# A two-layer hybrid decoder trunk: the instruction order comes from the framework's finer model, and layer 0's output projection multiplies three of its four chunk groups in three passes

## The chip, the cores and the metric

The kernel runs on one core of one Trainium2 chip. The metric is the device time of one execution in microseconds (us). The kernel before takes 2581.92 us, the median of three runs (2581.72 to 2582.03).

## What is computed

One sequence of 256 tokens, width 2048, goes through two layers. All arrays are float32. Each layer has a token mixer and a feed-forward part (FFN), both normalised and then shifted, scaled and gated by six vectors that a conditioning vector `c` gives. The mixer projects to 4888 columns, runs three mixers on their shares of the columns, and projects the joined results back.

```python
def reference(x, c, positions, w_mod, b_mod, ...):
    c_act = jax.nn.silu(c)
    for l in range(DEPTH):                                  # 2 layers
        mod = c_act @ w_mod[l] + b_mod[l]                   # 2048 x 12288 per layer
        shift1, scale1, gate1, shift2, scale2, gate2 = jnp.split(mod[:, None, :], 6, axis=-1)
        h = rms_norm(x, norm1_gain[l]) * (1.0 + scale1) + shift1
        x = x + gate1 * hybrid_token_mixer(h, ...)
        h = rms_norm(x, norm2_gain[l]) * (1.0 + scale2) + shift2
        x = x + gate2 * swiglu_ffn(h, ffn_w_gate[l], ffn_w_up[l], ffn_w_down[l])
    return rms_norm(x, final_norm_gain)

def hybrid_token_mixer(h, ..., w_in, ..., w_out):
    (aq, ak, av, ag, alr, bq, bk, bv, cq, ck, cv, cz, cb, ca) = _split_columns(h @ w_in, IN_SIZES)
    o_a = ...   # gated linear attention, 4 heads
    o_b = ...   # sliding-window softmax attention, 16 heads
    o_c = ...   # gated DeltaNet, 4 heads: short convolution, then a triangular solve per chunk
    return jnp.concatenate([o_a, o_b, o_c], axis=-1) @ w_out

def swiglu_ffn(h, w_gate, w_up, w_down):                    # 2048 -> 5632 -> 2048
    return (jax.nn.silu(h @ w_gate) * (h @ w_up)) @ w_down
```

## The kernel before

Everything is written once, unrolled, in one function `trunk`, about 18,400 instructions. The 256 tokens are two blocks (`blk`) of 128 rows. Each projection is a `stream` of jobs: a job is one row block `k` of 128 weight rows by up to 1024 columns. SyncE's queue (SP) loads it (`raw`, 512 KB, line 323); then there are two ways to multiply it.

- **Three passes.** ScalarE (ACT) copies `raw` to a rounded part `wh` (L330), VectorE (DVE) subtracts to get the remainder `wl` (L331), and TensorE (PE) multiplies the activations' parts `xh` and `xl` with them: three matmuls for each block and 512 columns (L358).
- **Whole.** The unsplit float32 row block is multiplied by unsplit float32 activations: one matmul in the program for each block and 512 columns, which the trace records as two. Nothing is split on ACT or DVE, and `raw` rotates through the nine buffers `raw`, `wh`, `wl` and not three.

`stream` chooses by the set `whole`:

```python
            if k in whole:
                terms = ((lhs(k, blk, True), 0),)
            else:
                xh, xl = lhs(k, blk, False)
                terms = ((xh, 0), (xh, 1), (xl, 0))
```

Layer 0's input projection is whole in all but 13 jobs of the columns from 0 and the 16 of the columns from 1024; layer 1 has nothing whole. The output projection has four groups of four row blocks: group 0 holds the gated linear attention (GLA), 1 and 2 the softmax attention, 3 DeltaNet. It first runs the row blocks 4 to 15 (groups 1 to 3), which do not need GLA, with GLA's own steps among them, and then the blocks 0 to 3. `to_mix` and `split_mix` keep a group's activations whole, or split them (ACT copy, DVE subtraction on L393), by `WHOLE_OUT[l]`.

**The modulation.** `mod = c_act @ w_mod` has one row, so it is not a matmul: SP loads 512 KB pieces (`mraw`, two buffers, L220) and DVE multiplies and adds each piece into `acc` (L223, 128x1024). The first pieces of layer 0, which the first normalisation needs, are 256 KB and go through the buffers `g`. A finished sum is turned by PE (L248) and DVE (L250 to L256) into columns, or by L238 into a gate's row. In the code, `tick` writes these pieces between the jobs, at rates set by constants, so the 448 pieces (320 of 512 KB, 128 of 256 KB) are spread over both layers.

**The DeltaNet recurrence.** For each of six sizes and two blocks there is a chain: PE L678, DVE L680, PE L685, DVE L686, PE L403 (transpose), ACT L687, and behind it further steps to L735. The softmax attention is L895, L898 to L906, L911, L916, L920 for each set of heads.

**What sets the order.** The code's order gives priorities only. The framework (`TileContext`) walks a model of the core and puts on each engine the ready instruction of highest priority, then writes the waits. Each engine, and SP's queue, has its own list in that order.

Of the kernel before, what the change touches and what calls it, by code (L numbers as in the profile page):

```python
# [42 lines left out]
WHOLE_IN = (True, False)  # L43
WHOLE_A = (3, 0)
RATE_LAST = 1.6
WHOLE_OUT = ((0, 1, 2, 3), ())
XN_ACT = ((False, False), (False, False))

FIN_LAG = 4
# [54 lines left out]
def trunk(ctx: ExitStack, tc, x, cT, pos, small, consts, b_mod, w_mod, w_in, w_gk, w_out,  # L104
# [272 lines left out]
    def ahead(wsp_n, hm_n):  # L377
        return (None,) * wsp_n + (at_hm,) * hm_n
# [7 lines left out]
    def split(src, scale=None):  # L386

        h = tl(hmp, [P, 4, P], "hm", F32R)
        lo = tl(hmp, [P, 4, P], "hm", F32R)
        h2, lo2 = (t.rearrange("p a b -> p (a b)") for t in (h, lo))  # L390
        if scale is None:
            A.activation(h2, src, AF.Copy)
            V.tensor_tensor(lo2, src, h2.bitcast(F32), ALU.subtract)  # L393
        else:
            A.activation(h2, src, AF.Copy, scale=scale)
            V.scalar_tensor_tensor(lo2, src, scale, h2.bitcast(F32), ALU.mult, ALU.subtract)
        return h, lo
# [91 lines left out]
    def to_mix(l, key, ps, gain=None):  # L489
        if key[1] == 0 and 0 not in WHOLE_OUT[l]:  # L490
            mix[key] = split(ps, gain)
            return
        t = mix[key] if key in mix else tl(hmp, [P, 4, P], "hm")
        A.activation(t.rearrange("p a b -> p (a b)"), ps, AF.Copy,
                     scale=1.0 if gain is None else gain)
        mix[key] = t
# [23 lines left out]
    def split_mix(l, group):  # L520
        if group not in WHOLE_OUT[l]:
            for blk in range(NB):
                mix[blk, group] = split(mix[blk, group].rearrange("p a b -> p (a b)"))
# [425 lines left out]
    def layer(l):  # L949
# [158 lines left out]
        for ks in (range(4, 16), range(0, 4)):  # L1108
            final = ks[0] == 0
            if final:  # L1110
# [3 lines left out]
                           blk, j, ps, half, final)) for half in range(2)]  # L1114
            stream(groups, ks, lhs_mix, whole=[k for k in ks if k // 4 in WHOLE_OUT[l]],
                   tail=() if not final else TAIL_WHOLE if 0 in WHOLE_OUT[l] else
                   ahead(*TAIL_OUT))
# [100 lines left out]
```

## Time and profile before

| | |
|---|---|
| median of three runs | 2581.92 us |
| the profiled execution | 2585.34 us, of which 2583.5 us are the span of instructions |
| PE busy | 2432.7 us (94%), 11,164 records |
| DVE busy | 1714.4 us (66%) |
| ACT busy | 1053.5 us (41%) |
| moved by DMA | 600.79 MB, 233 GB/s over the span |

The stages stand in the trace, by the first matmul of each, at: 40.8 us layer 0's input projection (the normalisation uses its first modulation before that); 238 us the columns that run beside DeltaNet's and the softmax attention's steps; 408 us layer 0's output projection with GLA; 566 us layer 0's FFN; 1372 us layer 1's mixer; 1816 us layer 1's FFN; the last matmul ends near 2566 us. The program has 10,120 matmuls and transposes on PE.

In the rows that follow, a busy share counts an engine's instructions; PEclk is the granted TensorE clock as a share of full speed, and the DMA share is the mean busy share of the core's 16 DMA engines.

### The profile page before, as it was taken

What the parts mean: (1) busy time and instruction counts of PE and PEld (TensorE: products, weight loads), DVE (VectorE), ACT (ScalarE), POOL (GpSimd) and SP (SyncE); (2) the same over time, 40 slices, a digit from 0 to 9 for tenths busy, and PEclk for the clock granted to TensorE, in tenths of its full rate; (3) what the DMA queues carried; (4) which work ended last, traced back from release to release, by engine and by line L of the source; (5) the groups of instructions that cost most, each with busy time, mean ns of one, the idle gap of its engine ahead of it and who ended that gap; (6) DMA issues with size and microseconds to landing.
All of it is one profiled execution on the core that took longest, in us unless ns stands there. A gap on an engine that the chain in (4) does not pass through costs nothing.

```text
span 2583.5 us, 30803 instructions
## 1 busy us (share of the span) xinstructions
PE 2432.7 (94%) x11164; PEld 1884.1 (73%) x11164; DVE 1714.4 (66%) x2171; ACT 1053.5 (41%) x1548; POOL 58.2 (2%) x117
## 2 busy tenths in 40 slices
PE   4999998889999988999999999999999999999998
PEld 2555785447878767788877878877778878888876
DVE  6767867576675777657578785888664575544555
ACT  2203443124444333344335454564644434344443
POOL 1000000000000000000000000000000000000000
PEclk9999999989999999999999999999999999999999
DMA  9996538777778888868687861675676686666654
GB/s 341 368 322 204 180 114 282 258 231 268 261 259 260 283 268 274 292 193 286 223 277 261 281 192 50 214 232 192 212 256 193 200 286 195 188 191 188 189 184 155
DMA packets 190033, 600.79 MB, mean 233 GB/s; under 512 B 21628, under 2 KB 26268, under 8 KB 189496
## 3 DMA queue, kind: packets, MB, share of 16 engines
q1 hardware_dynamic: 189880, 598.81, 70.7%
q8 instruction: 88, 1.44, 0.2%
q14 instruction: 65, 0.53, 0.1%
HBM read 596.63 MB, written 2.10 MB: 232 GB/s over the span
## 4 chain that ended last, share of the span: by engine, by line
PE 57%; DMA 20%; DVE 10%; issue 8%; ACT 4%; POOL 1%; SPq 1%; DVEq 0%; ACTq 0%; POOLq 0%
PE acc L358 48%; DMA mraw<-in_w_mod 13%; DVE wl L331 4%; DMA raw<-in_w_down 3%; DMA raw<-in_w_in 2%; DVE acc L223 2%; ACT wh L330 1%; PE mm L403 1%; PE ga L895 1%; DMA raw<-in_w_up 1%; PE mm L678 1%; PE mm L685 1%; PE ga L916 1%; DMA raw<-in_w_gate 1%; PE fin L248 1%
## 5 line engine op out<-in xcount | busy, mean ns | idle before, releaser
L358 PE MATMUL acc<-wh,hm 128*128 128x512 f32 (+3 forms) x4872 | 1339.2, 389 | 20.9 <-DVE xs L931 4.7
L330 ACT ACTIVATE wh<-raw 128x1024 fp32r<-128x1024 f32 (+3 forms) x669 | 684.7, 1025 | 985.8 <-PE acc L358 548.9
L331 DVE TENSOR_TENSOR wl<-raw,wh 128x1024 fp32r<-128x1024 f32 (+3 forms) x669 | 785.2, 1179 | 446.6 <-ACT wh L330 444.5
L358 PEld LDWEIGHTS acc<-wh,hm 128*128 128x128 f32 x4872 | 892.0, 189 | 215.8 <-issue 25.5
L358 PE MATMUL acc<-wl,hm 128*128 128x512 f32 (+3 forms) x2484 | 792.3, 394 | 12.2 <-DVE wl L331 9.7
L223 DVE SCALAR_TENSOR_TENSOR acc<-mraw,c_act,acc 128x1024 f32<-128x1024 f32 x320 | 410.3, 1282 | 225.2 <-DMA mraw<-in_w_mod 222.9
L358 PEld LDWEIGHTS acc<-wl,hm 128*128 128x128 f32 x2484 | 458.4, 190 | 124.1 <-DVE wl L331 22.3
L358 PE MATMUL acc<-wh,ahl 128*128 128x512 f32 x560 | 158.4, 397 | 0.0
L358 PEld LDWEIGHTS acc<-wh,ahl 128*128 128x128 f32 x560 | 105.8, 189 | 24.5
L358 PE MATMUL acc<-wl,ahl 128*128 128x512 f32 x280 | 90.8, 398 | 7.2 <-DVE wl L331 7.2
L223 DVE SCALAR_TENSOR_TENSOR g<-g,c_act,g 128x512 f32<-128x512 f32 x128 | 88.7, 747 | 12.6 <-DMA g<-in_w_mod 12.4
L358 PE MATMUL acc<-wh,b 128*128 128x512 f32 (+2 forms) x184 | 74.7, 545 | 2.2 <-ACT b L447 2.1
L358 PE MATMUL acc<-wl,b 128*128 128x512 f32 (+2 forms) x176 | 67.1, 518 | 2.6 <-DVE g L969 2.6
L358 PEld LDWEIGHTS acc<-wl,ahl 128*128 128x128 f32 x280 | 52.2, 189 | 23.1 <-DVE wl L331 11.3
L358 PE MATMUL acc<-raw,b 128*128 128x512 f32 (+2 forms) x176 | 67.6, 524 | 0.0
L358 PEld LDWEIGHTS acc<-wh,b 128*128 128x128 f32 x184 | 35.2, 197 | 30.8 <-issue 23.1
L358 PEld LDWEIGHTS acc<-wl,b 128*128 128x128 f32 x176 | 32.8, 192 | 29.2 <-issue 20.3
L416 ACT ACTIVATE acc<-xs 128x512 f32<-128x512 f32 x32 | 19.0, 595 | 85.7 <-DVE xs L931 85.7
L447 ACT ACTIVATE b<-mm,mod,mod 128x128 f32<-128x128 f32 x24 | 9.2, 461 | 109.7 <-DVE mod L256 92.1
L358 PEld LDWEIGHTS acc<-raw,b 128*128 128x128 f32 x176 | 33.5, 195 | 26.7 <-issue 21.7
L929 DVE TENSOR_TENSOR acc<-acc,gate 128x512 f32<-128x512 f32 x64 | 43.0, 695 | 10.3 <-PE acc L358 10.2
L358 PE MATMUL acc<-raw,hm 128*128 128x512 f32 x88 | 41.7, 598 | 1.4 <-ACT acc L416 1.4
(314 smaller groups left out, 1645.8 us busy)
## 6 DMA issues: line engine op xcount, KB each, us to landing
mraw<-in_w_mod SPq DMA_DIRECT2D x320, 512.0 KB
raw<-in_w_down SPq DMA_DIRECT2D x176, 512.0 KB
raw<-in_w_gate SPq DMA_DIRECT2D x160, 512.0 KB
raw<-in_w_up SPq DMA_DIRECT2D x160, 512.0 KB
raw<-in_w_in SPq DMA_DIRECT2D x72, 512.0 KB
g<-in_w_mod SPq DMA_DIRECT2D x128, 256.0 KB
raw<-in_w_out SPq DMA_DIRECT2D x43, 512.0 KB
raw<-in_w_in SPq DMA_DIRECT2D x32, 264.0 KB
```

Of the source, the lines that this page charges most:

```text
L223: V.scalar_tensor_tensor(acc, raw[:, a], c_act[:, i + a:i + a + 1], acc, ALU.mult, ALU.add)
L248: TE.transpose(ps[:, i * P:(i + 1) * P], acc[:, (j + i) * P:(j + i + 1) * P], ident)
L330: A.activation(wh[:, :width], raw[:, :width], AF.Copy)
L331: V.tensor_tensor(wl[:, :width], raw[:, :width], wh[:, :width].bitcast(F32), ALU.subtract)
L358: TE.matmul(ps[blk, j][:, :segs[j][2]], xa, parts[j][part], start=i == 0 and n == 0, stop=last and n == len(terms) - 1)
L403: TE.transpose(ps[:, j * P:(j + 1) * P], src[:, j * P:(j + 1) * P], ident)
L416: A.activation(scr[0]() if junk is None else junk, xs[:, blk, j * 512:(j + 1) * 512], AF.Square, accum_out=ssq[blk][:, j:j + 1])
L678: TE.matmul(ps[:, s], LT[blk][:, s], Tm[blk][:, s], start=True, stop=True)
L685: TE.matmul(ps[:, s], U[blk][:, s], m1[:, s], start=True, stop=True)
L895: TE.matmul(ps[:, j * nk:(j + 1) * nk], qT[rows, i + j], kT[rows, g, :nk], start=True, stop=True)
L916: TE.matmul(ps[:, j * 64:(j + 1) * 64], pT[:, j * nk + kb * P:j * nk + (kb + 1) * P], kv[kb][:, P + g * 64:P + (g + 1) * 64], start=kb == ...
L929: V.tensor_tensor(ps, ps, need(gate_row, (l, part, j)), ALU.mult)
```

## The change

Two edits. The order of all instructions now comes from the framework's other, finer model of the core. And in layer 0's output projection only group 0 (GLA) stays whole; the groups 1 to 3 take three passes, so 96 whole matmuls become 288, 24 jobs get a `wh` and a `wl`, and six activation tiles get a split.

```diff
--- before.py
+++ after.py
@@ -43,7 +43,7 @@
 WHOLE_IN = (True, False)
 WHOLE_A = (3, 0)
 RATE_LAST = 1.6
-WHOLE_OUT = ((0, 1, 2, 3), ())
+WHOLE_OUT = ((0,), ())
 XN_ACT = ((False, False), (False, False))
 
 FIN_LAG = 4
@@ -1211,7 +1211,7 @@
         args.append(nc.dram_tensor(f"in_{n}", a.shape, mybir.dt.from_np(a.dtype),
                                    kind="ExternalInput").ap())
     args.append(nc.dram_tensor("out_0", (T, D), F32, kind="ExternalOutput").ap())
-    with tile.TileContext(nc) as tc:
+    with tile.TileContext(nc, schedule_with_timeline_sim=True) as tc:
         trunk(tc, *args)
     r = run_bass_kernel_spmd(nc, [named], core_ids=[0])
     return r.results[0]["out_0"].reshape(1, T, D)
```

The edits' reach is seen in the order. On SP at the start of the program, before (`g` in L220: first modulation pieces, 256 KB; `wh_347`, `wl_372`: buffers that hold whole row blocks of the input projection, L323):

```order
L220 DMA g_295<-in_w_mod 128x512
L220 DMA g_298<-in_w_mod 128x512
L220 DMA g_301<-in_w_mod 128x512
L220 DMA g_313<-in_w_mod 128x512
L323 DMA wh_347<-in_w_in 128x1024
L213 DMA g_357<-in_b_mod 1x512
L220 DMA g_360<-in_w_mod 128x512
L213 DMA g_363<-in_b_mod 1x512
L220 DMA g_366<-in_w_mod 128x512
```

and now:

```order
L220 DMA g_232<-in_w_mod 128x512
L323 DMA wh_347<-in_w_in 128x1024
L323 DMA wl_372<-in_w_in 128x1024
L323 DMA raw_387<-in_w_in 128x1024
L323 DMA wh_402<-in_w_in 128x1024
L323 DMA wl_424<-in_w_in 128x520
L220 DMA g_235<-in_w_mod 128x512
L323 DMA raw_437<-in_w_in 128x520
L220 DMA g_238<-in_w_mod 128x512
L220 DMA g_241<-in_w_mod 128x512
L323 DMA wh_449<-in_w_in 128x520
L220 DMA g_244<-in_w_mod 128x512
```

Before, the first weight block followed the last of the 32 pieces that the first normalisation needs. Now ten weight loads, and a little later four 512 KB pieces of the first gate's modulation, are queued ahead of the last of them: 16.6 MB stand in the list up to that piece, 10.9 MB before.

On PE in layer 0's DeltaNet recurrence (L678, L685, L403), before (`acc` from `wh`, `wl`: the input projection's columns from 0; `ga` from `consts`: the softmax attention's transposes):

```order
L678 MATMUL mm_1719<-g_1693,g_1681 128x128 x4
L358 MATMUL acc_2497<-wh_2608,hm_993 128x512
L358 MATMUL acc_2498<-wh_2608,hm_993 128x512
L358 MATMUL acc_2493<-wh_2629,hm_657 128x512
L358 MATMUL acc_2494<-wh_2629,hm_657 128x512
L358 MATMUL acc_2493<-wl_2630,hm_657 128x512
L685 MATMUL mm_1726<-g_1724,g_1690 128x128 x4
L358 MATMUL acc_2494<-wl_2630,hm_657 128x512
L911 MATMUL ga_2191<-consts_88,b_2178 128x128 x2
L358 MATMUL acc_2493<-wh_2629,hm_658 128x512
L911 MATMUL ga_2191<-consts_88,b_2178 128x128 x2
L358 MATMUL acc_2494<-wh_2629,hm_658 128x512
```

and now:

```order
L678 MATMUL mm_1719<-g_1693,g_1681 128x128 x4
L895 MATMUL ga_2255<-kT_1425,b_2170 128x256 x2
L248 MATMUL fin_3783<-consts_88,acc_3481 128x128 x4
L685 MATMUL mm_1726<-g_1724,g_1690 128x128 x4
L248 MATMUL fin_3789<-consts_88,acc_3481 128x128 x4
L403 MATMUL mm_1732<-consts_88,g_1693 128x128 x4
L678 MATMUL mm_1738<-g_1650,g_1638 128x128 x4
L911 MATMUL ga_2266<-consts_88,b_2253 128x128 x4
L916 MATMUL ga_2272<-kv_533,b_2265 128x64
L916 MATMUL ga_2272<-kv_538,b_2265 128x64
L916 MATMUL ga_2272<-kv_533,b_2265 128x64
L916 MATMUL ga_2272<-kv_538,b_2265 128x64
```

The projection's matmuls have gone: they now stand ahead of the recurrence. Between the last matmul of the input projection and the first of the output projection there were 7 instructions on PE, and now there are 326; in layer 1, 6 and now 192.

On DVE at the same place, before:

```order
L680 TENSOR_TENSOR g_1724<-mm_1719,masks_90 128x512
L901 TENSOR_REDUCE low_590_2184<-b_2178 128x2
L223 SCALAR_TENSOR_TENSOR acc_2032<-mraw_2666,c_act_102,acc_2032 128x1024
L686 TENSOR_TENSOR g_1693<-g_1693,mm_1726 128x512
L906 RECIPROCAL tot_591_2186<-tot_591_2186 128x2
L331 TENSOR_TENSOR wl_2672<-raw_2669,wh_2671 128x1024
L223 SCALAR_TENSOR_TENSOR acc_2032<-mraw_2687,c_act_102,acc_2032 128x1024
L680 TENSOR_TENSOR g_1743<-mm_1738,masks_90 128x512
L920 TENSOR_TENSOR b_2177<-ga_2197,tot_591_2186 128x2x64
L223 SCALAR_TENSOR_TENSOR acc_2032<-mraw_2708,c_act_102,acc_2032 128x1024
```

and now:

```order
L680 TENSOR_TENSOR g_1724<-mm_1719,masks_90 128x512
L223 SCALAR_TENSOR_TENSOR acc_3691<-mraw_3694,c_act_102,acc_3691 128x1024
L898 TENSOR_TENSOR b_2253<-ga_2255,masks_90 128x2x256
L250 TENSOR_REDUCE sums_960_3782<-fin_3783 128x4
L686 TENSOR_TENSOR g_1693<-g_1693,mm_1726 128x512
L223 SCALAR_TENSOR_TENSOR acc_3691<-mraw_3715,c_act_102,acc_3691 128x1024
L901 TENSOR_REDUCE low_611_2259<-b_2253 128x2
L250 TENSOR_REDUCE sums_960_3782<-fin_3789 128x4
L223 SCALAR_TENSOR_TENSOR acc_3691<-mraw_3718,c_act_102,acc_3691 128x1024
L680 TENSOR_TENSOR g_1743<-mm_1738,masks_90 128x512
```

Modulation pieces (L223) now stand between almost all steps of the recurrence, 41 of them beside those 326 PE instructions; before, the steps shared DVE with fewer pieces and with the projection's splits (L331).

On SP in layer 0's FFN, at the loads of `w_down`, before:

```order
L220 DMA mraw_6710<-in_w_mod 128x1024
L323 DMA raw_6317<-in_w_down 128x1024
L220 DMA mraw_6767<-in_w_mod 128x1024
L323 DMA raw_6335<-in_w_down 128x1024
L220 DMA mraw_6806<-in_w_mod 128x1024
L323 DMA raw_6356<-in_w_down 128x1024
L323 DMA raw_6374<-in_w_down 128x1024
L220 DMA mraw_6863<-in_w_mod 128x1024
L323 DMA raw_6395<-in_w_down 128x1024
L220 DMA mraw_6902<-in_w_mod 128x1024
```

and now:

```order
L220 DMA mraw_8539<-in_w_mod 128x1024
L323 DMA raw_6590<-in_w_down 128x1024
L220 DMA mraw_8578<-in_w_mod 128x1024
L323 DMA raw_6611<-in_w_down 128x1024
L220 DMA mraw_8635<-in_w_mod 128x1024
L323 DMA raw_6629<-in_w_down 128x1024
L220 DMA mraw_8674<-in_w_mod 128x1024
L323 DMA raw_6647<-in_w_down 128x1024
L213 DMA acc_10057<-in_b_mod 1x1024
L323 DMA raw_6668<-in_w_down 128x1024
```

Pieces and weights now alternate one to one. Counted over SP's whole list, the 512 KB pieces stand as follows; the bytes in all are the same.

| stage (SP's list, from its first weight load) | before | now |
|---|---|---|
| layer 0 up to its output projection | 47 | 56 |
| layer 0's output projection | 42 | 40 |
| layer 0's FFN | 135 | 192 |
| layer 1's mixer | 64 | 0 |
| layer 1's FFN | 32 | 32 |

## The prediction

> **What bounds the kernel now.** I read the page's busy times, the windows by stage, the chain of waits, and the timeline at the places that the order moves. The page, and the chain's shares by engine:
>
> ```profile
> span 2583.5 us, 30803 instructions
> PE 2432.7 (94%) x11164; PEld 1884.1 (73%) x11164; DVE 1714.4 (66%) x2171; ACT 1053.5 (41%) x1548; POOL 58.2 (2%) x117
> PE 57%; DMA 20%; DVE 10%; issue 8%; ACT 4%; POOL 1%; SPq 1%; DVEq 0%; ACTq 0%; POOLq 0%
> by line: PE acc L358 48.4%; DMA mraw<-in_w_mod 12.7%; issue 7.9%; DVE wl L331 4.0%; DMA raw<-in_w_down 2.8%; DMA raw<-in_w_in 2.3%; DVE acc L223 2.1%; ACT wh L330 1.2%; PE mm L403 1.1%; PE ga L895 0.9%; DMA raw<-in_w_up 0.9%; PE mm L678 0.8
> ```
>
> PE is the bound where it is dense; where it waits, it mostly waits for modulation pieces (`mraw`), which no matmul reads but which stand in DVE's list and SP's list ahead of what one does read. The windows show which stage has room (columns: PE, PEld, DVE, ACT and POOL busy, granted clock, DMA share, GB/s):
>
> ```profile
> 36.00:165.00 129.00, 125.34 (x388) 70.06 (x388) 92.15 (x155) 20.43 (x48) 2.73 (x16) 1.00 1.01 365
> 220.00:410.00 190.00, 181.28 (x1083) 143.56 (x1082) 141.60 (x276) 88.36 (x202) 11.72 (x17) 0.96 0.52 165
> 408.00:558.00 150.00, 136.23 (x463) 66.01 (x463) 103.42 (x137) 27.44 (x57) 5.89 (x5) 0.98 0.82 274
> 558.00:566.00 8.00, 2.23 (x8) 1.43 (x8) 7.93 (x13) 4.27 (x11) 0.55 (x1) 0.71 0.80 272
> 566.00:1372.00 806.00, 768.68 (x3354) 617.38 (x3355) 543.38 (x522) 330.74 (x383) 10.00 (x12) 0.98 0.78 258
> 861.00:1016.00 155.00, 140.57 (x604) 110.68 (x603) 108.68 (x102) 53.63 (x53) 1.90 (x2) 0.99 0.84 275
> 1200.00:1245.00 45.00, 45.00 (x206) 37.24 (x205) 32.09 (x31) 19.34 (x21) 0.00 (x0) 1.00 0.86 286
> 1372.00:1816.00 444.00, 422.22 (x2434) 348.85 (x2434) 344.51 (x547) 233.53 (x431) 18.41 (x35) 0.99 0.62 200
> 1816.00:2566.00 750.00, 738.34 (x3265) 603.35 (x3264) 415.63 (x399) 324.73 (x370) 1.28 (x2) 1.00 0.65 206
> ```
>
> The start (36 to 165) is full of transfers: share 1.01. The recurrences of layer 0 (220 to 410) leave the DMA half empty, yet keep PE at 95%. The same FFN takes 806 us in layer 0, with 135 pieces, and 750 us in layer 1, with 32.
>
> **The passes.** In the timeline and in a dense stretch of the chain:
>
> ```profile
> 47.33 3.60 PE L358 MATMUL acc<-wl,b 128*128 128x512 f32 x8
> 50.76 3.60 PE L358 MATMUL acc<-raw,b 128*128 128x512 f32 x8
> 1112.83 50.38 PE acc L358 x222
> ```
>
> Eight records, that is four whole matmuls, start 3.43 us after the four before: 0.858 us each. A pass takes 50.38/222 = 0.227 us, three 0.681. So 96 x (0.858 - 0.681) = 17 us of PE go. The price is 24 more ACT copies and DVE subtractions of a row block and six of an activation tile:
>
> ```profile
> L330 ACT ACTIVATE wh<-raw 128x1024 fp32r<-128x1024 f32 x605 | 640.5, 1060 | 918.6 <-PE acc L358 526.0 <-DMA raw<-in_w_down 118.8 <-DMA raw<-in_w_up 104.6
> L331 DVE TENSOR_TENSOR wl<-raw,wh 128x1024 fp32r<-128x1024 f32 x605 | 736.7, 1223 | 435.6 <-ACT wh L330 434.3
> ```
>
> A job now holds PE for 12 x 0.227 = 2.7 us; 1.06 us of ACT and 1.22 us of DVE hide under that, and DVE gets rid of this stage's pieces. The tile splits fall among the last DeltaNet steps. GLA's end loses cover: its last normalisation now has eight whole matmuls beside it, where more stood before. These small losses and the pieces' absence I set against each other: -18 us for the stage, between -30 (its 14 us of idle PE go too) and 0 (GLA's chain becomes the bound).
>
> **The start.** DVE and SP there:
>
> ```profile
> 5.32 26.05 SPq L220 DMA_DIRECT2D g<-in_w_mod  x31
> 26.89 9.56 DVE L223 SCALAR_TENSOR_TENSOR g<-g,c_act,g 128x512 f32<-128x512 f32 x14 [0.38 <-DMA g<-in_w_mod]
> 35.72 1.12 PE L248 MATMUL fin<-consts,g 128*128 128x128 f32 x4 [16.02 <-DVE g L223]
> 40.83 2.08 PE L358 MATMUL acc<-wh,b 128*128 128x512 f32 x2 [2.09 <-ACT b L447]
> ```
>
> The first matmul waits for the last of 32 pieces. That piece now stands at 16.6 MB of SP's list and not at 10.9: 5.7 MB at 365 GB/s are 15.5 us, so L248 comes at 51 and the first matmul at 56. The weights that came early are needed soon after, but the four gate pieces are not. The four row groups take (238 - 40.8)/4 = 49 us of PE each. The pieces for groups 2, 3 and 4 now end at 36.0, 55.2 and 66.5 MB (before 25.6, 39.1, 52.8): landed by 105, 157 and 188 us, and usable 5 us later. PE is ready for them at 105, 159 and 211, so two short waits come on top: +21 us at the end of the stage, between +5 (DVE's four extra pieces alone, 1.3 us each) and +35.
>
> **Layer 0's recurrence.** The projection's matmuls stood in its gaps; they now run ahead, dense. I price PE's operations by their start-to-start times in this trace: 151 us for the stage now (147 before), of which 61 us are the 326 instructions that stand alone. Before, it lasted 238 to 408, 170 us. The dense part is then 90 us, and 7 more for DVE, which has convolutions, rotations and splits there. The bare part has 41 pieces in DVE's list between the steps. How fast pieces come when two buffers are all there is shows in the chain at 174 us:
>
> ```profile
> 173.97 4.09 DMA mraw<-in_w_mod
> 178.16 1.30 DVE acc L223
> 179.47 4.00 DMA mraw<-in_w_mod
> 183.56 1.30 DVE acc L223
> 184.88 3.95 DMA mraw<-in_w_mod
> ```
>
> One buffer goes round in 5.45 us, so a piece comes every 2.7 us and 41 take 111 us. A second route is the chain itself:
>
> ```profile
> 296.32 0.69 DVE L680 TENSOR_TENSOR g<-mm,masks 128x512 f32<-128x512 f32 x1 [1.02 <-PE mm L678]
> 301.71 0.69 DVE L680 TENSOR_TENSOR g<-mm,masks 128x512 f32<-128x512 f32 x1
> 307.25 0.69 DVE L680 TENSOR_TENSOR g<-mm,masks 128x512 f32<-128x512 f32 x1 [0.39 <-PE mm L678]
> ```
>
> A step took 5.4 us with matmuls and pieces between; 12 steps are 65 us, and the steps ahead and behind come to some 40. So 97 + 113 = 210 us against 170: +40 us, between +8 (the bare part at 80 us, if pieces never gate a step) and +65. What hid here was the projection's work; nothing covers the steps now. The page "DMA: Bandwidth & Descriptors" of the Trainium skill, in "Anatomy of one DMA", fits a transfer as 2.0 us plus its bytes at 436 GB/s; 512 KB would then land in an estimated 3.2 us, a piece would come every 2.25 us, 41 in 92 us, and the term would be +19. The rows above have 4.0 us, and decide.
>
> **Layer 0's FFN.** Its 264 weight loads are 138 MB. With 135 pieces it moved 209 MB in 806 us (258 GB/s, the row above); with 192 it has to move 239. Where pieces were dense, from 861 to 1016, PE waited at 275 GB/s; from 1200 to 1245 it did not wait at 286. At 275 the stage takes 869 us (+63), at 286 836 (+30). I take the middle, +45, since the `w_down` loads of the first rate and the gate and up loads of the second both get more pieces: between -5 and +85.
>
> **Layer 1.** Its mixer loses all 64 pieces (82 us of DVE, 34 MB), but 192 PE instructions (37 us) of its recurrence stand alone too. PE's work there is 401 us of 444; I expect 10 us won ahead of the recurrence, 15 of idle lost in it, 10 won behind, hence about -4, between -25 and +15. The FFN keeps 32 pieces, only packed closer: +3.
>
> **Sum.** 21 + 40 - 18 + 45 - 4 + 3 = 87 us. The profiled execution took 2585.3 us (2 us of it around the span), 3.4 over the median of 2581.9; I add to the median: 2669 us.
>
> **The rivals.**
> - *The FFN takes its 57 pieces for nothing.* For it: 286 GB/s without a wait. Against it: 861 to 1016. Without that term: 2624 us.
> - *Faster: an even alternation ends the FFN's waits.* Before, pieces come in bursts; one piece to each weight block could let layer 0's FFN run like layer 1's: 750 us and not 806, -56 in place of +45, in all 2568 us. It decides from an FFN of 761 us down. Against it: 239 MB in 750 us are 319 GB/s, which the FFN's windows above do not reach.
> - *Longer: the FFN holds 258 to 268 GB/s or the recurrence costs +65.* 239 MB at 263 GB/s take 909 us, +103 and not +45: 2727 us.
> - *Colder matmuls in the bare stretches.* The granted clock falls where PE idles: 0.71 from 558 to 566. If a third of the 61 us of bare matmuls runs at half speed and on the path, 20 us more, 2689. The page "TensorE: Matmul & The Clock Gate" of the Trainium skill, Part 1, says that an idle window of about 3.4 us halves the clock; by that rule the gaps of some 2 us between steps would mostly not trip it.
> - That the order changes nothing is excluded: the lists differ at each place.
>
> **How the numbers follow.** Runs of this kernel tell 0.2% (5 us) from no change. My forecast with its neighbours, 2635 to 2705 (the colder matmuls, 0.1, lie inside): 0.45. The FFN for nothing, 2598 to 2635: 0.17. Longer: 0.24, of which 0.07 beyond 2745. Faster: 0.10. Between 2577 and 2598: 0.04, of which 0.03 within 0.2%. The range 2598 to 2745 leaves out 0.21. Slower by over 0.2%: 0.87; faster 0.10; same 0.03.
>
> **What the profile after would show.** First matmul near 56 us. From about 350 to 470 us a stretch with PE about half busy, DVE waiting for `mraw`. Layer 0's output projection in some 140 us. Layer 0's FFN at 840 to 870 us with about 280 GB/s. Layer 1's mixer without L223, near 440 us. Wrong would be the sum if the FFN holds over 300 GB/s, or if the bare stretch takes under 90 us.

## The result: 4.8% slower, and the profile after

The changed kernel takes 2704.41 us (median of four runs, 2701.4 to 2709.78) against 2581.82 us in the same comparison: a ratio of 1.0483, 95% interval 1.046 to 1.0505, or 122.6 us more. The prediction's 2669 us was 35 us short; 2704 lies within its range. The profiled execution took 2701.4 us, 3.0 under the median of its kernel, the one of before 3.5 over its own, so the traces differ by 116 us only.

The page of the changed kernel: span, busy times, and the granted clock and the GB/s in forty slices of 67.5 us.

```profile
span 2699.5 us, 31228 instructions
PE 2470.5 (92%) x11260; PEld 1960.5 (73%) x11260; DVE 1751.6 (65%) x2201; ACT 1085.3 (40%) x1581; POOL 54.8 (2%) x117
PEclk9999988899999999899999999988999999999999
GB/s 359 359 328 230 221 242 186 102 120 193 298 301 326 316 313 301 306 324 344 252 208 158 178 189 111 79 78 103 164 302 284 187 187 171 175 200 187 187 187 148
```

PE is busy 38 us longer, although by the prediction's count the passes take 17 us of work from it. The granted clock goes with that: it lies between 0.8 and 0.9 (digit 8) in the three slices from 337 to 540 us. The transfers show the pieces' new places: 298 GB/s and more in layer 0's FFN from 675 to 1282 us, under 112 in layer 1's recurrence.

The stages of the changed kernel (windows; columns as in the prediction):

```profile
36.00:55.00 19.00, 2.23 (x8) 1.43 (x8) 18.07 (x27) 0.51 (x2) 1.05 (x2) 1.00 1.03 385
258.00:369.00 111.00, 101.86 (x554) 81.80 (x551) 89.58 (x156) 60.67 (x114) 7.22 (x8) 0.94 0.71 230
369.00:495.00 126.00, 89.82 (x507) 77.61 (x508) 93.43 (x141) 34.75 (x94) 6.99 (x11) 0.78 0.58 168
495.00:628.00 133.00, 123.28 (x545) 88.30 (x543) 77.43 (x118) 53.41 (x91) 2.56 (x3) 0.96 0.39 123
628.00:1461.00 833.00, 776.74 (x3385) 628.20 (x3386) 623.91 (x597) 336.23 (x396) 14.61 (x29) 0.97 0.84 289
1461.00:1924.00 463.00, 433.34 (x2407) 364.08 (x2407) 269.76 (x475) 231.20 (x423) 11.12 (x18) 0.96 0.42 124
1924.00:2688.00 764.00, 747.15 (x3284) 611.52 (x3282) 414.70 (x395) 322.53 (x367) 1.31 (x3) 0.99 0.63 201
```

The row that stands out is 369 to 495: PE busy for 71% at a clock of 0.78, DVE for 74%. (The input projection's last matmul ends at 362.6 us, so the bare stretch, in which the recurrence's instructions stand alone on PE, is 363 to 495.) Layer 1's mixer got longer although its DVE work fell from 345 to 270 us.

All stages of all kernels, read from the traces by the first matmul of each stage, in us. "Head" is from the first matmul to layer 0's FFN: row groups, DeltaNet and softmax attention, output projection with GLA. FFN 1 ends with its last matmul, before the change at 2572.5 us; the 750 us that the prediction has for it stop 6 us earlier. The ratio is to the kernel before in the same comparison, with its 95% interval.

| kernel | ratio | first matmul | head | FFN 0 | mixer 1 | FFN 1 |
|---|---|---|---|---|---|---|
| before | | 40.8 | 525 | 806 | 444 | 756 |
| after | 1.0483 (1.046 to 1.0505) | 55.0 | 573 | 832 | 463 | 765 |
| E1 order only | 1.053 (1.0502 to 1.0557) | 55.7 | 581 | 838 | 465 | 766 |
| E2 passes only | 1.0022 (1.0008 to 1.0036) | 41.4 | 526 | 807 | 446 | 756 |
| E3 few pieces, after | 1.0234 (1.0212 to 1.0256) | 53.6 | 513 | 835 | 464 | 764 |
| E4 few pieces, before | 0.9873 (0.9854 to 0.9892) | 40.9 | 497 | 794 | 447 | 758 |
| E5 start put back | 1.0415 (1.0394 to 1.0435) | 39.8 | 572 | 837 | 464 | 758 |
| E6 96 pieces held | 1.0545 (1.0524 to 1.0566) | 55.2 | 575 | 801 | 513 | 766 |
| E7 three buffers, after | 1.0156 (1.0137 to 1.0175) | 57.4 | 542 | 783 | 462 | 764 |
| E8 three buffers, before | 0.9902 (0.9883 to 0.9921) | 40.2 | 507 | 794 | 449 | 753 |
| E9 recurrence tied | 1.0554 (1.0533 to 1.0575) | 55.7 | 595 | 837 | 479 | 757 |
| E10 tied, three buffers, start | 1.036 (1.034 to 1.0381) | 39.9 | 590 | 783 | 491 | 762 |
| E11 passes, three buffers | 0.9938 (0.9913 to 0.9962) | 40.6 | 524 | 782 | 449 | 756 |
| E12 softmax on two banks | 1.0427 (1.041 to 1.0444) | 54.4 | 557 | 823 | 485 | 764 |

### The profile page after: what moved, and what is told of

Same layout as the page of the kernel before. It is cut to its first block, busy times and chain, and to the rows that moved or that the text cites. A ratio compares the mean times of both kernels' runs of the same rounds, so it can differ in the third digit from the quotient of the medians.

```text
span 2699.5 us, 31228 instructions
## 1 busy us (share of the span) xinstructions
PE 2470.5 (92%) x11260; PEld 1960.5 (73%) x11260; DVE 1751.6 (65%) x2201; ACT 1085.3 (40%) x1581; POOL 54.8 (2%) x117
## 4 chain that ended last, share of the span: by engine, by line
PE 42%; DMA 9%; DVE 6%; ACT 3%; issue 2%; SPq 0%; POOL 0%; ACTq 0%; DVEq 0%; POOLq 0%
PE acc L358 38%; DMA mraw<-in_w_mod 5%; DVE wl L331 2%; DVE acc L223 1%; ACT wh L330 1%; DMA raw<-in_w_up 1%; DMA raw<-in_w_down 1%; DMA raw<-in_w_gate 1%; DVE acc L929 1%; DMA raw<-in_w_in 1%; PE mm L403 1%; PE ga L895 0%; PE ga L916 0%; PE ga L403 0%; PE mm L678 0%
## 5 line engine op out<-in xcount | busy, mean ns | idle before, releaser
L358 PE MATMUL acc<-wh,hm 128*128 128x512 f32 (+3 forms) x5000 | 1385.4, 389 | 27.5 <-DVE xs L931 18.8
L331 DVE TENSOR_TENSOR wl<-raw,wh 128x1024 fp32r<-128x1024 f32 (+3 forms) x693 | 815.0, 1181 | 551.1 <-ACT wh L330 548.1
L330 ACT ACTIVATE wh<-raw 128x1024 fp32r<-128x1024 f32 (+3 forms) x693 | 709.3, 1027 | 1008.5 <-PE acc L358 537.3
L358 PEld LDWEIGHTS acc<-wh,hm 128*128 128x128 f32 x5000 | 929.4, 191 | 222.0 <-issue 24.3
L358 PE MATMUL acc<-wl,hm 128*128 128x512 f32 (+2 forms) x2516 | 811.3, 391 | 10.9 <-DVE wl L331 9.5
L358 PEld LDWEIGHTS acc<-wl,hm 128*128 128x128 f32 x2516 | 471.7, 191 | 114.4 <-DVE wl L331 18.2
L223 DVE SCALAR_TENSOR_TENSOR acc<-mraw,c_act,acc 128x1024 f32<-128x1024 f32 x320 | 410.1, 1282 | 150.2 <-DMA mraw<-in_w_mod 148.2
L223 DVE SCALAR_TENSOR_TENSOR g<-g,c_act,g 128x512 f32<-128x512 f32 x128 | 89.7, 746 | 17.8 <-DMA g<-in_w_mod 12.2
L358 PE MATMUL acc<-raw,b 128*128 128x512 f32 (+2 forms) x176 | 73.5, 527 | 1.5 <-ACT b L447 1.5
L358 PE MATMUL acc<-wl,b 128*128 128x512 f32 (+2 forms) x176 | 73.2, 526 | 1.5 <-ACT b L447 1.5
L931 DVE TENSOR_TENSOR xs<-xs,acc 128x512 f32<-128x512 f32 x64 | 41.5, 679 | 0.2
L248 PE MATMUL fin<-consts,g 128*128 128x128 f32 x32 | 6.5, 337 | 37.4 <-DVE g L223 35.0
```

The lines of the kernel that those rows point to most:

```text
L223: V.scalar_tensor_tensor(acc, raw[:, a], c_act[:, i + a:i + a + 1], acc, ALU.mult, ALU.add)
L248: TE.transpose(ps[:, i * P:(i + 1) * P], acc[:, (j + i) * P:(j + i + 1) * P], ident)
L330: A.activation(wh[:, :width], raw[:, :width], AF.Copy)
L331: V.tensor_tensor(wl[:, :width], raw[:, :width], wh[:, :width].bitcast(F32), ALU.subtract)
L358: TE.matmul(ps[blk, j][:, :segs[j][2]], xa, parts[j][part], start=i == 0 and n == 0, stop=last and n == len(terms) - 1)
L931: V.tensor_tensor(x_j, x_j, ps, ALU.add)
```

## The experiments

The edits are given in short form.

### E1 and E2: each edit alone

```diff
 E1, in the changed kernel            E2, in the kernel before
-WHOLE_OUT = ((0,), ())              -WHOLE_OUT = ((0, 1, 2, 3), ())
+WHOLE_OUT = ((0, 1, 2, 3), ())      +WHOLE_OUT = ((0,), ())
```

> The finer model's order with the output projection of layer 0 left whole, as before. The list of PE now has 24 whole matmuls of the output projection (20.6 us at 0.858 us) between the first and the last step of layer 0's DeltaNet recurrence, where the changed kernel has none. Theory (pieces of the modulation gate the recurrence, the passes are a separate gain): recurrence and output projection of layer 0 together 360 to 390 us, against 370 in the changed kernel; all other stages as in the changed kernel; total 2690 to 2720 us. Rival (the passes cost the recurrence its cover): both stages together near 330 us as before, total near 2665 us.

> The order of before, with layer 0's output projection in three passes for the softmax attention's and DeltaNet's chunks. Theory (the passes are worth their 17 us of PE work wherever they stand): 2564 us, the output projection at 140 us instead of 158, all else as before. Rival (the stage is bound by pieces and GLA's chain, the shorter matmuls only wait longer): 2580 us, the same as before.

The order alone costs 5.3% (2717.57 us), so the order accounts for all of the loss. In E1 the 24 whole matmuls stand among the recurrence, and the head takes 581 us, 7 more than with the passes: the rival, that they cover the recurrence, falls. E1's theory held (2690 to 2720 us).

The passes alone give nothing: 2588.06 us, 0.2% slower, the rival's case. E2's output projection takes 163 us, not 140. The waits of E2 in that stage point at a price that I had left out (total us, times, longest):

```profile
ACT wh L330 <- DMA raw<-in_w_out: 54.9, 18, 7.0
PE acc L358 <- DVE wl L331: 6.7, 5, 4.4
PE ga L823 <- DVE a L804: 10.3, 5, 3.2
```

18 times ACT waits for a weight block, 54.9 us in all. Whole blocks rotate through nine buffers; split ones through the three of `raw`, so fewer loads run ahead: when the second half of the columns begins, 4 of its 12 blocks have been issued, before the change 8. ACT's waits are not all on the path: PE itself waits 7 us for a split and 10 us for GLA's steps on DVE (2.5 before).

### E3 and E4: the pieces taken out of layer 0's head

```diff
+        cut = l == 0 and part in (GATE1, SHIFT2, SCALE2)
-        return [((l, part), lambda i=i: step(i)) for i in range(0, KD, rows)]
+        return [((l, part), lambda i=i: step(i)) for i in range(0, rows if cut else KD, rows)]
```

> The changed kernel with 90 of the 96 pieces of layer 0's first gate, second shift and second scale left out (each of their six sums takes one row block of sixteen), so no piece stands in the recurrence, in the output projection or before them. Theory (pieces in DVE's list gate the bare recurrence): from the end of the row groups to the output projection 165 to 185 us instead of 236; the FFN of layer 0 and layer 1 as in the changed kernel; total 2610 to 2640 us. Rival (the bare chain of steps, with cold matmuls, sets the length): 215 us or more for that stretch, total 2670 us or more.

> The kernel before with the same 90 pieces left out: the control. Theory: the order matters less without pieces; 2540 to 2560 us, the recurrence stage 150 to 165 us instead of 170, the output projection 145 us instead of 158. The changed kernel without these pieces then stands 55 to 90 us behind it (FFN of layer 0, layer 1 and some 15 us of bare chain). Rival (bare chain): 110 us or more behind it.

From the end of the row groups to the output projection E3 takes 178.7 us where the changed kernel takes 236.5; with the same pieces left out, the kernel before goes from 170.3 to 162.4. So the pieces cost the new order 58 us there and the old one 8; of the 66 us by which the change lengthens this stretch, 16 remain without pieces (178.7 against 162.4). The steps show a part of how. DVE's L680, of before, of the changed kernel and of E3 (count, duration in ns, first and last start):

```profile
L680 DVE TENSOR_TENSOR g<-mm,masks x12: 684/692/692, 289.7 to 346.2; 128x512 f32<-128x512 f32 x12
```
```profile
L680 DVE TENSOR_TENSOR g<-mm,masks x12: 680/683/692, 384.0 to 458.6; 128x512 f32<-128x512 f32 x12
```
```profile
L680 DVE TENSOR_TENSOR g<-mm,masks x12: 684/692/693, 344.0 to 400.0; 128x512 f32<-128x512 f32 x12
```

A step takes 5.1 us before the change (56.5/11), 6.8 in the changed kernel, and 5.1 again in E3, whose list still has 246 bare instructions. In layer 0, bare steps alone are not slower; steps with pieces between them are. The steps are 19 of the 58 us (74.6 us from the first to the last start, 56.0 in E3). 32 us arise ahead of the first step, which comes 125 us after the row groups' end and in E3 94, and 8 behind the last. The pieces of the changed kernel from 320 us on and, of these, in the bare stretch, and what DVE waited for from 320 us on:

```profile
L223 DVE SCALAR_TENSOR_TENSOR acc<-mraw,c_act,acc x54: 1262/1283/1286, 320.3 to 478.9; 128x1024 f32<-128x1024 f32 x54
L223 DVE SCALAR_TENSOR_TENSOR acc<-mraw,c_act,acc x41: 1262/1283/1286, 361.9 to 478.9; 128x1024 f32<-128x1024 f32 x41
DVE acc L223 <- DMA mraw<-in_w_mod: 28.3, 37, 2.0
```

41 pieces ran in the bare stretch, one in 2.9 us. The clock goes with the pieces in large part: it is 0.78 in the bare stretch of the changed kernel and 0.91 in E3's:

```profile
363.00:495.00 132.00, 92.91 (x515) 79.27 (x516) 96.28 (x145) 40.62 (x107) 6.99 (x11) 0.78 0.60 177
```
```profile
354.50:429.00 74.50, 59.02 (x405) 49.71 (x403) 35.32 (x74) 31.78 (x89) 3.14 (x7) 0.91 0.05 17
```

E3's total came out 1 us over the theory's 2640; against E4 it stands 92 us behind, 2 us outside the theory's 55 to 90. What remains in the head without pieces, 513 against 497 us, E12 takes up.

### E5: the start put back

```diff
-                SY.dma_start(raw[:, o:o + m], w[...])
+                d = SY.dma_start(raw[:, o:o + m], w[...])
+                if l == 0 and first: tc.keep_in_program_order(d)
...
+                if l == 0 and last: hold[:] = [h[1][1][1][:, 0, 0:1]]   # the next piece waits for group 2
```

> The changed kernel, with the weight loads of the first row group kept behind the 32 pieces that the first normalisation needs, and the first gate's pieces held until the second row group is normalised. The last of the 32 pieces then stands at 10.9 MB of SP's list, as before the change (16.6 MB in the changed kernel). Theory (the start pays for the bytes ahead of that piece, and gets nothing back): first matmul at 41 us instead of 55, the four row groups 197 to 204 us, and the gain of 14 us stays to the end: 2682 to 2694 us. Rival (the weights that came early save as much later): first matmul at 41 us, but the row groups end at 255 us or later and the total stays above 2698 us.

The first matmul is back at 39.8 us and the whole is 2689.95 us, 14 less than the changed kernel. The theory held: the 5.7 MB ahead of the last early piece cost their transfer time and gave nothing back.

### E6: 96 pieces held back from layer 0's FFN

```diff
+                if l and blk: hold[:] = [h[1][3][1][:, 0, 0:1]]   # the next piece waits for layer 1's activations
```

> The changed kernel, with the last 96 pieces of layer 1 that it runs in layer 0's FFN held until layer 1's first activations are there. Layer 0's FFN has 96 pieces instead of 192, layer 1's mixer 96 instead of none. Theory (each piece in the FFN costs its share of the transfers, (832 - 765)/(192 - 32) = 0.42 us): layer 0's FFN at 790 to 800 us instead of 832; layer 1's mixer loses that and more, since 23 of the pieces fall into its bare recurrence: 495 to 525 us instead of 463; total 2695 to 2735 us. Rival (the finer order itself makes the FFN slower, pieces or not): layer 0's FFN stays over 820 us.

The FFN falls to 801 us (theory 790 to 800, rival over 820), 0.32 us a piece; the mixer grows by 50 us to 513, and the whole to 2723.18. Pieces cost 0.3 us in a dense stage and 0.5 in a mixer with bare steps.

### E7 and E8: a third buffer for the pieces

```diff
-    modp = ctx.enter_context(tc.tile_pool(name="modp", bufs=2))
+    modp = ctx.enter_context(tc.tile_pool(name="modp", bufs=3))
-        pb = bs.enter_context(tc.tile_pool(name=f"swa_{l}", bufs=9, ...
+        pb = bs.enter_context(tc.tile_pool(name=f"swa_{l}", bufs=8, ...
```

> The changed kernel with three buffers for the modulation's pieces instead of two; the softmax attention's tiles get eight buffers instead of nine to make room. 77 pieces stand ahead of the output projection instead of 56, and 10 instead of 34 between the recurrence's first and last step on DVE. Theory (the round trip of two buffers gates DVE's list, and with it the steps): from the end of the row groups to the output projection 175 to 200 us instead of 236, waits of DVE for pieces there under half of before; total 2650 to 2690 us. Rival (pieces cost DVE time and bytes, whatever the buffers): that stretch over 215 us or the gain is lost at the start, total over 2695 us.

> The kernel before with the same three buffers (and eight for the softmax attention). Theory (part of the chain's wait for pieces is the round trip of two buffers): layer 0's FFN 785 to 800 us instead of 806, total 2545 to 2572 us. Rival (the wait is for bytes, which more buffers don't change): within 6 us of before.

E7 takes 2621.8 us: 83 us of the loss go by one buffer more, beyond the theory's range. E8 takes 2556.61 us, within its theory, 1% less than before and the fastest kernel here with all pieces. In E7 the stretch from the row groups to the output projection is 209 us (theory 175 to 200, rival over 215): between the two; the steps are back at 5.0 us, the first one comes 124 us after the row groups' end, as late as in the changed kernel. The larger part came where I had not looked for it, in layer 0's FFN. Waits of DVE for pieces there, the changed kernel and E7, and E7's window:

```profile
DVE acc L223 <- DMA mraw<-in_w_mod: 87.6, 94, 3.8
```
```profile
  DMA mraw<-in_w_mod: 4.3, 8
600.00:1383.00 783.00, 762.47 (x3379) 621.24 (x3378) 621.76 (x595) 335.02 (x393) 14.63 (x29) 0.99 0.85 307
```

The same 192 pieces stand in that FFN. With three buffers DVE waits 4 us for them and not 88, and the stage moves 307 GB/s in 783 us, 23 us less than before the change with 135 pieces.

### E9 and E10: the steps among the projection again

In both layers, on PE, each row block of the input projection's last columns is tied behind the recurrence's instruction that it stood behind before the change; E10 adds E5 and E7.

```diff
+                if pace: tc.add_manual_dep(mm.ins, steps[pace[i] - 1].name, NoSync)   # order on PE, no wait
```

> The changed kernel, with the input projection's last columns of both layers tied to the recurrence: on PE each of their row blocks may not stand ahead of the recurrence's instruction that it stood behind before the change. No instruction of the recurrence stands alone any more (0 and 4 between the two projections, 326 and 192 in the changed kernel); the finer model again orders all else, 59 pieces now fall into the columns' stage and none into the output projection. Theory (the bare steps cost their cover, with pieces or without): layer 1's mixer, which has no pieces, 430 to 448 us instead of 463; layer 0 from the row groups to the FFN 335 to 355 us instead of 370; the rest as in the changed kernel; total 2660 to 2680 us. Rival (pieces in DVE's list are the whole cost, bare steps are free): layer 1's mixer stays over 458 us and layer 0 over 362 us.

> The changed kernel with four things together: the tied recurrence, three buffers for pieces (eight for the softmax attention), the weights behind the first normalisation's pieces, and the first gate's pieces held until the second row group. Theory (the four costs add up): the time with three buffers alone, 2622 us, less 17 at the start, 5 to 10 in the row groups, 10 to 20 in layer 0's recurrence and 15 to 25 in layer 1's: 2550 to 2575 us, so at or under the kernel before with three buffers (2557 us). Rival (the gains overlap, since each takes idle time that another takes too): over 2590 us.

Both rivals won. With no bare instructions left, layer 0's head is longer (595 us) and layer 1's mixer too (479, without one piece): 2728.77 us in all. E10 comes to 2678.38, 57 us more than three buffers alone. The model ordered much else anew, so this is not the cover alone. In E9 the row groups end 200 us after the first matmul, as in the changed kernel (203), but the first tied column comes 26 us later (23 in E10), because the steps that it stands behind come late. From the row groups' end to the output projection E9 takes 258 us, the changed kernel 237, and its steps, covered but with pieces between them, take 7.9 us each (7.0 in E10). So covering the steps in this way won nothing, and the costs do not add up as E10's theory had it.

### E11: the passes with three buffers

```diff
 E8 and:
-WHOLE_OUT = ((0, 1, 2, 3), ())
+WHOLE_OUT = ((0,), ())
```

> The kernel before with three buffers for pieces, and layer 0's output projection in three passes as in the change. Theory (the passes gave nothing with two buffers because pieces held DVE's list in that stage; with three buffers they pay): the output projection 126 to 133 us instead of 143, total 2540 to 2549 us. Rival (GLA's chain and the splits set that stage): 2553 us or more, no gain over three buffers alone (2557 us).

2569.18 us, not better than E8: the rival. The whole stage takes 162 us in place of 143. The first half of the output projection is done after 50 us in place of 67; then no matmul of the projection runs for 9 us, and the second half takes 73 in place of 46. E11's waits (the third is SP's queue, at pieces whose buffer DVE has not freed) and its window from the end of the first half and, last, E8's second half:

```profile
ACT wh L330 <- DMA raw<-in_w_out: 41.9, 10, 7.5
PE acc L358 <- ACT wh L330: 11.5, 5, 4.0
SPq L220 <- DVE acc L223: 49.6, 23, 12.4
452.00:534.00 82.00, 58.21 (x229) 43.30 (x230) 63.32 (x78) 18.08 (x34) 5.76 (x4) 0.77 0.71 237
```
```profile
471.00:517.00 46.00, 43.48 (x114) 19.84 (x113) 29.69 (x33) 0.21 (x1) 1.90 (x2) 1.00 0.89 309
```

PE works 95% of E8's stretch at full clock and 71% of E11's at 0.77: the split row blocks come late, as in E2. When the second half begins, 3 of its 12 blocks have been issued, in E8 7, and between the others SP waits 50 us for the pieces' buffers and 7 for those of weight blocks. Which of the two, the fewer buffers or the pieces between the loads, decides was not tried.

### E12: the softmax attention on two PSUM banks

The softmax attention's twelve sets of heads a layer (the expectation says double sets) use one bank, `ga`, three times each; GLA, behind them, uses the same. L898, one for each set, in layer 1, before and after:

```profile
L898 DVE TENSOR_TENSOR b<-ga,masks x12: 686/693/694, 1555.1 to 1669.6; 128x512 f32<-128x512 f32 x12
```
```profile
L898 DVE TENSOR_TENSOR b<-ga,masks x12: 683/693/694, 1624.7 to 1791.7; 128x512 f32<-128x512 f32 x12
```

A set takes 10.4 us before and 15.2 after, although the stage has no piece any more. DeltaNet's steps are slower there too, 6.2 us for 4.7 (L680 in layer 1, before and after):

```profile
L680 DVE TENSOR_TENSOR g<-mm,masks x12: 682/691/693, 1547.4 to 1599.1; 128x512 f32<-128x512 f32 x12
```
```profile
L680 DVE TENSOR_TENSOR g<-mm,masks x12: 679/691/692, 1679.5 to 1747.7; 128x512 f32<-128x512 f32 x12
```

So the new order slows both chains without any piece. The timeline of one set shows where it waits:

```profile
1706.32 0.59 PE L895 MATMUL ga<-kT,b 64*128 64x256 f32 x2
...
1709.44 0.19 ACT L904 ACTIVATION_READ_ACCUMULATOR b<-b,low 128x1 f32 x1
...
1710.62 0.66 PE L358 MATMUL acc<-wh,hm 128*128 128x264 f32 x4
...
1711.49 0.38 PE L911 MATMUL ga<-consts,b 128*128 128x128 f32 x2
...
1713.05 0.58 ACT L912 ACTIVATE b<-ga 128x512 f32<-128x512 f32 x1
...
1713.82 1.06 PE L678 MATMUL mm<-g,g 128*128 128x128 f32 x8
...
1715.81 1.00 PE L916 MATMUL ga<-kv,b 128*128 128x64 f32 x8
```

ACT has done its part at 1709.6 and 1713.6 us, and the set's next instruction on PE comes 1.9 and 2.2 us later, behind passes of the projection and a DeltaNet step that stand ahead of it in the list. In a set of before, L911 starts 0.1 us after the first half of L904 and L916 0.1 us after L912:

```profile
1602.14 0.19 ACT L904 ACTIVATION_READ_ACCUMULATOR b<-b,low 128x1 f32 x1
1602.39 0.43 PE L911 MATMUL ga<-consts,b 128*128 128x128 f32 x2
...
1605.21 0.59 ACT L912 ACTIVATE b<-ga 128x512 f32<-128x512 f32 x1
1605.89 1.06 PE L916 MATMUL ga<-kv,b 128*128 128x64 f32 x8
```

GLA starts late (L747, before and after; the output projection's first matmul is at 1693.8 and 1774.6):

```profile
L747 PE MATMUL ga<-consts,hm x8: 270/344/418, 1690.3 to 1696.9; 128*128 128x128 f32 x8
```
```profile
L747 PE MATMUL ga<-consts,hm x8: 351/421/477, 1798.4 to 1801.7; 128*128 128x128 f32 x8
```

```diff
                 pT = tl(pool, [P, 512], "b")
-                ps = bank("ga")
+                ps = tl(psf, [P, 512], "fin")
...
                 A.activation(pT, ps, AF.Copy)
-                ps = bank("ga")
+                ps = tl(psf, [P, 512], "fin")
```

> The changed kernel, with the softmax attention's transposes and second products in the PSUM bank of the modulation's ends (fin) and only its scores in the bank ga, so that one set of heads can begin while the one before it still holds a bank. The finer model then puts 7 pieces of the modulation between the row groups and the output projection of layer 0 (28 in the changed kernel) and 30 into layer 1's output projection (none). Theory (the softmax attention, a chain of twelve double sets through one bank, sets the end of the bare stretch, and GLA in the same bank can only start behind it): in layer 1, where no piece stands among the steps, a double set takes 10.5 to 12.5 us instead of 14.4, GLA starts less than 15 us behind the first matmul of the output projection (24 now), and the mixer takes 435 to 455 us instead of 463 despite its 30 pieces; total 2640 to 2685 us. Rival (the order of the lists alone sets the sets' pace, the bank does not matter): 13.5 us or more for a double set in layer 1 and a mixer of 460 us or more.

The sets are faster, the mixer is not. L898, L747 and L223 in E12's layer 1:

```profile
L898 DVE TENSOR_TENSOR b<-ga,masks x12: 681/683/694, 1606.1 to 1743.0; 128x512 f32<-128x512 f32 x12
L747 PE MATMUL ga<-consts,hm x8: 272/374/474, 1750.3 to 1760.7; 128*128 128x128 f32 x8
L223 DVE SCALAR_TENSOR_TENSOR acc<-mraw,c_act,acc x29: 1267/1284/1286, 1761.7 to 1868.3; 128x1024 f32<-128x1024 f32 x29
```

A set takes 12.4 us by these starts, and GLA starts 11 us ahead of the output projection instead of 24 behind it. But 29 pieces now run among GLA's steps, which last 132 us instead of 89, and the mixer takes 485 us, not 435 to 455; the whole 2691.89, not 2640 to 2685. In layer 0 the stretch up to the output projection falls from 236.5 to 186.1 us; the output projection then takes 167 and not 133.

## Why the prediction was right and where it was not

The sign, the places and five of six terms' signs were right. The terms, in us of the profiled executions:

| term | forecast | measured |
|---|---|---|
| start and row groups | +21 | +21 |
| layer 0's recurrence | +40 (8 to 65) | +66 |
| layer 0's output projection | -18 (-30 to 0) | -25 |
| layer 0's FFN | +45 (-5 to 85) | +26 |
| layer 1's mixer | -4 (-25 to 15) | +19 |
| layer 1's FFN | +3 | +9 |
| sum | +87 | +116 |

The total was nearer than its terms, by luck: layer 0's recurrence and layer 1's mixer were 49 us too small together, layer 0's output projection and FFN 26 too large. 2704.41 us lies just under the upper edge of the forecast with its neighbours, 2635 to 2705.

**Start: right, by its own steps.** First matmul 55.0 us (56 foretold), 258.7 for the end of the row groups (259); E5 undid it.

**Layer 0's recurrence: the mechanism right, the term 26 too small.** Pieces in DVE's list gate this stretch (58 us, E3), as foretold. By the prediction's own parts, the dense one took 104 us and not 97 (258.7 to 362.6; as long in E3, so not by pieces), the bare one 133 and not 113, a figure for which its two routes gave 111 and 105. The pieces were counted right, 41, and their price was near: 117 us, one in 2.9 and not 2.7. The step that failed is that the last piece was taken for the end: 16 us of the chains follow it (478.9 to 495.2). The second route was short as well: steps at 6.8 us and not 5.4, and 51 us ahead of them and behind, not 40. PE was busy for 70% of the bare stretch, not half. "Nothing covers the steps now" can stand for at most the 16 us that remain without pieces: bare steps keep 5.1 us (E3), and covered ones, with pieces between them, won nothing (E9). By the formula of the Trainium skill's page "DMA: Bandwidth & Descriptors" ("Anatomy of one DMA") the term would have been +19. The page fits it to transfers that GpSimd issues, and SP issues these; the trace, with a piece in 2.9 us and +66, does not come out by it.

**The output projection: the size near, the reason wrong.** I gave -17 to the passes. Alone they are worth nothing (E2: 163 us for 158), with three buffers for the pieces they cost 19 us in this stage (E11). The prediction let ACT's and DVE's splits hide under the matmuls; it did not ask when a split gets its row block, with three buffers in place of nine and pieces between the loads. On the new order the passes bring 7 us of head (E1 against the changed kernel). That the stage still fell by 25 goes with its pieces: after 478.9 us none ran until 650, in the FFN, and the recurrence paid for them. E4 agrees: with all blocks whole and no piece, the stage takes 137 us, 21 less than before.

**Layer 0's FFN: the sign right, 19 too much, and the wrong limit.** I priced bytes at 275 GB/s. What bound the stage was the round trip of two piece buffers, which I had used for the recurrence and not here: with three, 307 GB/s pass (E7). Even E7's 783 us do not reach the 761 from which the rival of an even alternation would have decided.

**Layer 1's mixer: the sign wrong, 4 beyond the upper end.** I priced the recurrence's bare matmuls (10, 15 and 10 us, which make -5 and not -4). Up to the output projection the stage is 8 us shorter, as its missing pieces suggest; the output projection, with GLA in it, is 26 us longer (149 for 123). The step that failed is "10 won behind": the softmax attention's sets and DeltaNet's steps are slower without any piece, and GLA starts 24 us behind the projection's first matmul, before the change 4 ahead of it. That the bank has a part in the sets' pace E12 shows (12.4 us for 15.2); the part of PE's list is read from one set of the timeline. How much of the 19 us goes by either is open: E12 changed the pieces too. I had not followed the softmax attention or GLA as chains at all.

**Layer 1's FFN**, +9 for +3, wasn't tried; its cause stays open.

**Colder matmuls** came, as one rival had it: 0.78 from 369 to 495 us. In the bare stretch without pieces it is 0.91 (E3), so most of the fall comes with them and belongs to the recurrence's 66 us, not to a term beside it; its own share stays open. The rule of the Trainium skill's page "TensorE: Matmul & The Clock Gate" (Part 1), an idle window of about 3.4 us, I had read as one that gaps of some 2 us "would mostly not trip". The longest waits of PE from 369 to 495 are these:

```profile
PE mm L685 <- DVE g L680: 7.8, 4, 3.8
PE ga L911 <- ACT b L904: 7.5, 3, 4.0
```

Only these two kinds have a wait of 3.4 us or more, and the clock still lost 22%: by single waits, my reading of that rule gave too little.

## What to carry to other kernels

When an order comes from a model, follow each serial chain (here DeltaNet's steps, the softmax attention's sets, GLA) through the engines' lists and take its pace from the trace; the same background work cost 58 us in one order and 8 in the other. Ask also what runs after the last piece of that work, and which chain starts late behind a slow one. Read a wait for a transfer as a question of buffers before one of bandwidth: the third buffer was worth 83 us on the new order and 26 on the old. And price a cheaper instruction with what has to arrive for it: the passes were to save 17 us of PE and gave nothing alone, where their splits waited for row blocks that came through three buffers in place of nine.

## What the runs showed of the hardware that was not expected

- The core's transfers, 258 GB/s before and 275 where PE waited, go on at 307 GB/s for 783 us in E7, beside 99% of the full TensorE clock.
- The same matmul can take up to twice as long in the gaps of a chain. L685 in the changed kernel, in ns (least, median, most), and, last, in E3, without pieces:

```profile
L685 PE MATMUL mm<-g,g x80: 275/275/553, 384.9 to 446.3; 128*128 128x128 f32 x80
```
```profile
L685 PE MATMUL mm<-g,g x80: 270/275/377, 347.9 to 394.1; 128*128 128x128 f32 x80
```
